# A transformer block in fp32 products: the last modulation group moved into the first down projection, and seven stages of block products in the second

## The chip, the cores and the metric

The kernel runs on one core of a Trainium2 chip. The metric is the device time of one launch in microseconds (us): three runs of the kernel before took 1014.57, 1015.23 and 1015.83, median 1015.23. Names used below: TensorE (PE) multiplies, VectorE (DVE) and ScalarE (ACT) work elementwise, GpSimd (POOL) does little here, SyncE (SP) issues the DMA transfers.

## The reference

One layer over 512 tokens of width 1024: a feed-forward half-step, a token mixer, a second feed-forward half-step. Each is modulated by shift, scale and gate vectors that come from a small vector `c` through a 1024 x 9216 matrix `w_ada`. Everything is float32.

```
sc = jax.nn.silu(c)
mod = sc @ w_ada[l] + b_ada[l]
sh1, s1, g1, sh2, s2, g2, sh3, s3, g3 = jnp.split(mod, N_MOD, axis=-1)
h = _modulate(x, sh1, s1)
x = x + 0.5 * g1[:, None, :] * _swiglu(h, ffn1_w_in[l], ffn1_w_out[l])
h = _modulate(x, sh2, s2)
y = _hybrid_mixer(h, ...)
x = x + g2[:, None, :] * y
h = _modulate(x, sh3, s3)
x = x + 0.5 * g3[:, None, :] * _swiglu(h, ffn2_w_in[l], ffn2_w_out[l])
```

`_modulate` is an RMS norm over the features, times (1 + scale), plus shift. `_swiglu` is `(silu(h @ Wg) * (h @ Wu)) @ w_out` with an inner width of 2816; the second product is the down projection.

## The kernel before

Activations are kept transposed: `xT` is 8 tiles of 128 features x 512 tokens, and the inner activations `act` are 22 tiles (k = 0 to 21) of 128 x 512. A float32 product is made of three matmuls (`mm3`, L475 to L477): each operand is split into a high and a low part, and high x high, high x low and low x high are summed in PSUM. The splits are made by ScalarE (the high part: `ah` of an activation, `wh` of a weight) and VectorE (the low part: `al`, `wl`; L919, L235, L275). Activations that have not been split yet are plain tiles, "whole".

The program has these stages: feed-forward 1, its down projection (`down`, from L1017), the mixer, feed-forward 2, its down projection (`last_down`, from L1152). A down projection makes the 8 tiles of the output, t = 0 to 7, each a sum over 22 k; the weights come in units of 8, 8 and 6 k (`KPARTS`). The update adds the product, times the gate, to `xT[t]` (L1026 in `down`, L1161 in `last_down`; both STT on VectorE).

**Seven stages.** Where two output tiles and 8 k are taken together, a Strassen-Winograd scheme does the 2 x 2 x 2 block product with seven products instead of eight. `seven_down` makes one stage: 7 products of 4 k, each k three matmuls of 128 x 256, that is 84 matmuls. It needs sums and differences of the weights (`sevenths`: in a stage 3 weight remainders of 128 x 1024 and 5 operations of 128 x 512 on VectorE) and of the activations (`act_sums`, L1127 for the differences and L1477 for their low parts: 16 of 128 x 256 and 8 of 128 x 512 for 8 k). These are made of whole activations. In the kernel before, `act[0:8]` are kept whole beside their halves (`self.whole`), and `act[8:16]` exist as high and low parts only: `whole()` in `act_sums` adds them up again (L1133, 8 of them).

**The order of the second down projection** is written out in `PLAN`. Its entries are "all" (all 22 k of a tile), "tail" (only the last 6 k), "most" (the first 8 and the last 6 k), and (0, t) or (1, t): a seven stage over k 0 to 7 or 8 to 15 for tiles t and t+1. Before: tiles 0 and 1 in full, tails of 4 to 7, the stages (0, 4) and (0, 6), tiles 2 and 3 as "most", the stages (1, 2), (1, 4) and (1, 6). Finished tiles are transposed back and stored (`store`, L1294), in between the other work.

**The modulation vectors** beyond the first ones are made in groups of up to four chunks of 512 columns of `w_ada` (`ada_sums`). A chunk is 8 loads of 128 x 512 (256 KB each, issued by SP) and 8 operations of VectorE that multiply by `sc` and add up (L826 for the first, L828 for the 7 others) into a tile `aa`. When a group's chunks are there, `ada_columns` adds over the partitions with one matmul per chunk against ones (L885; each writes 32 rows of one PSUM tile `pb`), ScalarE copies the result (`rw`, L888), after a step TensorE transposes it (L892), and VectorE adds the bias (L896) into `mod`. `ada_rest(groups)` yields after each pair of loads and products, so that the caller can lay it between other work: `side.step(n)` goes n steps on. Group 1 and 2 are made in the first down projection, group 3 (2 chunks: 16 loads, 16 operations of VectorE) in the second, where only its vectors are used.

**The end of the first down projection.** Tile 7 is done in two halves of 256 tokens (`ha`, `hb`), in written order (`in_order`), and the norm of the next stage is begun inside it: ScalarE squares `xT` (L739), VectorE adds the squares to `na` (L741), and six matmuls into the second half TensorE adds `na` over the partitions (L761). Instructions of one engine run in the order in which they stand.

Of the kernel before, what the change touches and what calls it, by code (L numbers as in the profile page):

```python
# [32 lines left out]
PLAN = (("all", 0), ("all", 1), ("tail", 4), ("tail", 5), ("tail", 6), ("tail", 7), (0, 4), (0, 6), ("most", 2), ("most", 3),  # L33
        (1, 2), (1, 4), (1, 6))
MISSING = {"all": (), "most": (1,), "tail": (0, 1)}
# [64 lines left out]
class Block:  # L100
# [814 lines left out]
    def glu_parts(self, a, late=False):  # L915
        nc = self.nc
        ah, al = self.slot(F32R, "ah", late), self.slot(F32R, "al", late)
        nc.scalar.copy(ah, a)
        nc.vector.tensor_tensor(out=al, in0=a, in1=ah.bitcast(F32), op=ALU.subtract)  # L919
        return ah, al  # L920
# [53 lines left out]
    def by_sevens(self, act, fs, others=()):  # L974
# [27 lines left out]
        def parted():  # L1002
            for i in range(last):
                act[i] = self.glu_parts(act[i], 8 <= i < 14)
                yield

        side.add(parted())
        for f in range(last, FT):
            p = []
            for _ in range(2):  # L1010
                u, q = self.next_unit(), self.acc()
                for k in (0, 4):
                    self.dense(q, u, self.h, k0=k, k1=k + 4)
                    side.step(3)
                p.append(q)
            act.append(self.glu(*p))
        self.splits = side  # L1017

    def down(self, act, gate, norm=None):

        nc = self.nc
        accum = self.slot(s="na") if norm else None
# [6 lines left out]
        def finish(t, ts, p):  # L1029
            update(t, ts, p)  # L1030
            if norm:
                self.square_in(t, ts, accum)

        def parts(t, ts, units=None, by=8, late=False):
# [6 lines left out]
            if late:  # L1041
                held.append((t, ts, p))
            elif norm and ts != full:
                update(t, ts, p)
            else:
                finish(t, ts, p)

        last = KT - 1
        side, held = Side(), []
        side.add(self.ada_rest((1, 2) if norm else (3,)))  # L1050
        if norm:
            self.consts = Side()
            self.consts.add(self.mixer_consts())

        def split_first():
# [8 lines left out]
            if norm:  # L1064
                finish(0, full, p)
            else:
                held.append((0, full, p))

        for t in range(last):
            if norm and t == 1:  # L1070
                self.masks()
            for i, _ in enumerate(parts(t, full, late=not norm and t < 2) if t else split_first()):
# [4 lines left out]
                if not norm and t > 2:  # L1077
                    if i == 1:
                        self.store(t - 2, range(NB))
                elif not norm and t == 2:  # L1080
                    if i == 0:
                        side.flush()
                        for h in held:
                            finish(*h)
                    elif i == 1:
                        self.store(0, range(NB))
        units = [self.next_unit(ahead=0) for _ in KPARTS]
        if not norm:
            for i, _ in enumerate(parts(last, ha, units)):
                if i < 2:  # L1090
                    self.store(last - 2 + i, range(NB))
            for i, _ in enumerate(parts(last, hb, units)):
                if i == 1:
                    self.store(last, range(2))
            self.store(last, range(2, 4))
            return None
# [26 lines left out]
    def act_sums(self, tiles):  # L1123
# [5 lines left out]
        def whole(x):  # L1129
            if not isinstance(x, tuple):  # L1130
                return x
            a = self.slot(s="aw")
            tt(out=a, in0=x[0].bitcast(F32), in1=x[1].bitcast(F32), op=ALU.add)  # L1133
# [18 lines left out]
    def last_down(self, act, gate):  # L1152

        nc = self.nc
        full = slice(0, NT)
        side, sums, parts7, ended, held = Side(), Side(), Side(), [], []
        side.add(self.ada_rest((3,)))
# [10 lines left out]
        def stores():  # L1168
            while ended:
                self.store(ended.pop(0), range(NB))  # L1170
                yield

        for at, (kind, t) in enumerate(PLAN):
            after = [k for k, _ in PLAN[at + 1:at + 3]] + ["all"] * 2
            if kind in SEVENS:
# [13 lines left out]
            p = self.acc()  # L1189
            for i, (k0, n) in enumerate(KPARTS):  # L1190
                if i in MISSING[kind]:
                    continue
                u = self.next_unit(ahead=0 if i == 2 and after[0] in SEVENS else 1)
                if kind == "tail" and after[0] == "tail" and after[1] in SEVENS or (
                        i == (0 if kind == "most" else 1) and after[0] in SEVENS):
                    ahead()
                if at == 2:
                    side.flush()
                for k in range(0, n, 2):
                    while not at and any(not isinstance(a, tuple) for a in act[:k0 + k + 5]):  # L1200
                        self.splits.step()
                    for j in range(k, k + 2):
                        xh, xl = act[k0 + j]
                        self.mm3(p, u[0][:, j, :], u[1][:, j, :], xh, xl, k0 + j == (16 if kind == "tail" else 0),
                                 k0 + j == FT - 1)
                    if at == 1:
                        side.step()
                    if at > 1 or i == 2 and at:
                        sums.step()
                    parts7.step()  # L1210
                if ended and kind != "tail":
                    self.store(ended.pop(0), range(NB))
            held.append((t, p))
            if at > 1:
                for h, p in held:
                    update(h, full, p)
                    if kind == "all" or h < 2:
                        ended.append(h)
                held = []
# [80 lines left out]
    def ffn2(self, norms):  # L1300
# [14 lines left out]
        self.by_sevens(act, SEVEN[1])  # L1315
# [1210 lines left out]
```

## Time and profile before

| | before |
|---|---|
| median of 3 runs | 1015.23 us (1014.57 to 1015.83) |
| the profiled execution's own time | 1016.3 us |
| its span in the trace | 1014.6 us |
| TensorE busy | 1003.9 us, 99% of the span |
| VectorE busy | 814.8 us, 80% |
| ScalarE busy | 521.2 us, 51% |
| granted TensorE clock, mean | 1.00 |
| first down projection, tile 5 to the norm's first sum | 332.26 to 373.23 |
| second down projection, first matmul to start of the last seven | 888.70 to 998.57 |

Times in the trace count from the span's start. In the lines that the prediction shows, a window gives its length and then the busy time of each engine with its number of instructions; a row of a timeline gives start, duration, engine, line, operation, and output <- inputs, with xN for N neighbours drawn together, and in brackets how long the engine had been idle and what released it. A row of a group gives count, busy time, mean duration in ns, and the idle time ahead of it. An operation's name stands without its buffer number.

### The profile page before, as it was taken

Reading aid. Unit: us, or ns where it says so; the run is one execution under the profiler, and the core shown is the slowest. Engines: PE = TensorE matmul, PEld = TensorE weight load, DVE = VectorE, ACT = ScalarE, POOL = GpSimd, SP = SyncE. Lnnn points to the kernel's source line nnn. Section 1 sums busy time; section 2 is a strip of 40 time slices with the busy share of each in tenths; the row PEclk is TensorE's granted clock in tenths of the full one; section 3 lists DMA queues with packets and bytes.
Section 4 is the critical chain, followed back from the end, with each engine's and each line's share of the span. In section 5 each row is a group of like instructions: output and inputs, shape, how many; then the busy total and the mean of one; then the engine's idle time right before and its main releaser. Section 6 shows DMA issues by size and latency. Waiting matters only on the chain.

```text
span 1014.6 us, 17859 instructions
## 1 busy us (share of the span) xinstructions
PE 1003.9 (99%) x7029; PEld 906.2 (89%) x7029; DVE 814.8 (80%) x1445; ACT 521.2 (51%) x942; POOL 30.6 (3%) x74
## 2 busy tenths in 40 slices
PE   7999999999999999999999999999999999999998
PEld 6788999999887899888888888999999999987988
DVE  4779999887797847778987649789888888788995
ACT  4454555556422225658756365375555555634443
POOL 0000000000200000100001012000000000000000
PEclk9999999999999999999999999999999999999999
DMA  9863564334588825321132021212333434372612
GB/s 319 295 202 101 170 205 144 107 108 117 172 306 286 299 65 165 102 61 44 48 77 69 24 63 43 83 49 83 99 111 98 116 93 121 107 259 65 177 42 63
DMA packets 204034, 130.84 MB, mean 129 GB/s; under 512 B 14497, under 2 KB 188590, under 8 KB 203950
## 3 DMA queue, kind: packets, MB, share of 16 engines
q1 hardware_dynamic: 203950, 129.70, 42.0%
q8 instruction: 55, 0.90, 0.3%
q14 instruction: 29, 0.24, 0.1%
HBM read 127.18 MB, written 2.49 MB: 128 GB/s over the span
## 4 chain that ended last, share of the span: by engine, by line
PE 92%; DVE 4%; DMA 1%; ACT 1%; SPq 1%; issue 1%; POOL 0%; DVEq 0%; ACTq 0%
PE pa L360 18%; PE pa L475 14%; PE pa L477 14%; PE pa L476 14%; PE pb L360 13%; PE pa L1244 3%; PE pb L1244 2%; DMA ar<-in_w_ada 1%; PE pb L2212 1%; SPq L139 1%; PE pb L475 1%; PE pb L476 1%; PE pb L477 1%; PE pb L2192 1%; PE pb L1749 1%; DVE cv L1693 1%
## 5 line engine op out<-in xcount | busy, mean ns | idle before, releaser
L275 DVE TENSOR_TENSOR wl<-wr,wh 128x1024 fp32r<-128x1024 f32 x114 | 138.6, 1220 | 34.7 <-ACT wh L279 34.4
L234 ACT CAST wh<-wr 128x1024 fp32r<-128x1024 f32 (+1 forms) x81 | 81.0, 1009 | 131.6 <-PE pa L476 118.2
L279 ACT CAST wh<-wr 128x1024 fp32r<-128x1024 f32 x114 | 116.6, 1051 | 22.4 <-DVE wr L275 19.9
L235 DVE TENSOR_TENSOR wl<-wr,wh 128x1024 fp32r<-128x1024 f32 (+1 forms) x81 | 94.1, 1167 | 37.4 <-ACT wh L234 36.1
L475 PE MATMUL pa<-hh,wh 128*128 128x512 f32 (+1 forms) x309 | 119.2, 386 | 0.0
L477 PE MATMUL pa<-hh,wl 128*128 128x512 f32 (+1 forms) x309 | 116.2, 376 | 0.0
L476 PE MATMUL pa<-hl,wh 128*128 128x512 f32 (+1 forms) x309 | 116.1, 376 | 0.0
L475 PE MATMUL pa<-ah,wh 128*128 128x512 f32 (+1 forms) x294 | 110.5, 376 | 0.0
L476 PE MATMUL pa<-al,wh 128*128 128x512 f32 (+1 forms) x294 | 110.0, 374 | 0.0
L477 PE MATMUL pa<-ah,wl 128*128 128x512 f32 (+1 forms) x294 | 109.7, 373 | 0.0
L275 DVE TENSOR_TENSOR wr<-wr,wr 128x512 f32<-128x512 f32 x114 | 78.4, 688 | 1.7
L828 DVE SCALAR_TENSOR_TENSOR aa<-ar,sc,aa 128x512 f32<-128x512 f32 x98 | 73.4, 749 | 7.7 <-DMA ar<-in_w_ada 6.0
L360 PE MATMUL pa<-th,wh 128*128 128x256 f32 x264 | 74.8, 283 | 0.2 <-ACT z L365 0.2
L360 PE MATMUL pa<-hh,wh 128*128 128x256 f32 x264 | 74.8, 283 | 0.0
L360 PE MATMUL pa<-hh,wl 128*128 128x256 f32 x264 | 74.7, 283 | 0.0
L360 PE MATMUL pa<-tl,wh 128*128 128x256 f32 x264 | 74.7, 283 | 0.0
L360 PE MATMUL pa<-th,wl 128*128 128x256 f32 x264 | 74.7, 283 | 0.0
L360 PE MATMUL pa<-hl,wh 128*128 128x256 f32 x264 | 74.7, 283 | 0.0
L475 PEld LDWEIGHTS pa<-hh,wh 128*128 128x128 f32 x309 | 58.4, 189 | 10.1 <-issue 1.6
L477 PEld LDWEIGHTS pa<-hh,wl 128*128 128x128 f32 x309 | 58.2, 188 | 10.1
L475 PEld LDWEIGHTS pa<-ah,wh 128*128 128x128 f32 x294 | 55.3, 188 | 12.2 <-ACT wh L234 2.5
L476 PEld LDWEIGHTS pa<-hl,wh 128*128 128x128 f32 x309 | 58.4, 189 | 8.5
(488 smaller groups left out, 2694.3 us busy)
## 6 DMA issues: line engine op xcount, KB each, us to landing
wr<-in_ffn_w_in SPq DMA_DIRECT2D x79, 512.0 KB
ar<-in_w_ada SPq DMA_DIRECT2D x128, 256.0 KB
wr<-in_ffn_w_out SPq DMA_DIRECT2D x32, 512.0 KB
wr<-in_w_in SPq DMA_DIRECT2D x21, 512.0 KB
wr<-in_ffn_w_out SPq DMA_DIRECT2D x16, 384.0 KB
wr<-in_w_out SPq DMA_DIRECT2D x8, 512.0 KB
wr<-in_ffn_w_in SPq DMA_DIRECT2D x8, 384.0 KB
ar<-in_w_ada SPq DMA_DIRECT2D x6, 512.0 KB
```

What stands on the lines that cost most here:

```text
L139: return self.nc.sync.dma_start(dst, src)
L234: self.nc.scalar.copy(hi, raw)
L235: self.nc.vector.tensor_tensor(out=lo, in0=raw, in1=hi.bitcast(F32), op=ALU.subtract)
L275: sub = lambda out, x, y: nc.vector.tensor_tensor(out=out, in0=x, in1=y, op=ALU.subtract)
L279: nc.scalar.copy(hi[:, :n], raw[:, :n])
L360: nc.tensor.matmul(z, a[:, j, :], b, start=start and j == 0 and i == 0, stop=j == 3 and i == 2, skip_group_check=not start)
L475: mm(out, wh, xh, start=start, stop=False)
L476: mm(out, wh, xl, start=False, stop=False)
L477: mm(out, wl, xh, start=False, stop=stop)
L828: nc.vector.scalar_tensor_tensor(out=acc, in0=a, scalar=sc, in1=acc, op0=ALU.mult, op1=ALU.add)
L1244: nc.tensor.matmul(z, a[:, j, :], b, start=start and j == 0 and i == 0, stop=j == 3 and i == 2, skip_group_check=not start)
L1693: nc.vector.scalar_tensor_tensor(out=a[:, d:], in0=p[:, :NT - d], scalar=wj(3 - d), in1=a[:, d:], op0=ALU.mult, op1=ALU.add)
```

## The change

Three things are changed.

1. Group 3 of the modulation vectors is made in `down` (first down projection), behind groups 1 and 2, and no longer in `last_down`. There the rate of the steps goes from 2 to 3 from tile 4 on. `down` has lost its branch for a second down projection, which nothing called.
2. `PLAN` of the second down projection: "head" (the first 8 k) of tiles 0 and 1, tails of 0, 1 and 2, the stages (0, 2), (0, 4), (0, 6), tails of 3 to 7, the stages (1, 0), (1, 2), (1, 4), (1, 6). That is seven stages instead of five; "all" and "most" are gone. A tile's head and its tail are one sum in PSUM (`begun`).
3. `act[8:16]` stay whole (`left`). Their high and low parts are made between the products of the (0, t) stages (`second`), for the first four of them only the first 256 tokens, since the (1, t) stages need no more of them; the eight additions of `whole()` are gone.

```
-PLAN = (("all", 0), ("all", 1), ("tail", 4), ("tail", 5), ("tail", 6), ("tail", 7), (0, 4), (0, 6), ("most", 2), ("most", 3),
-        (1, 2), (1, 4), (1, 6))
+PLAN = (("head", 0), ("head", 1), ("tail", 0), ("tail", 1), ("tail", 2), (0, 2), (0, 4), (0, 6), ("tail", 3), ("tail", 4),
+        ("tail", 5), ("tail", 6), ("tail", 7), (1, 0), (1, 2), (1, 4), (1, 6))
...
+    def glu_parts(self, a, late=False, ts=slice(0, NT)):
...
+        nc.scalar.copy(ah[:, ts], a[:, ts])
+        nc.vector.tensor_tensor(out=al[:, ts], in0=a[:, ts], in1=ah[:, ts].bitcast(F32), op=ALU.subtract)
...
             for i in range(last):
-                act[i] = self.glu_parts(act[i], 8 <= i < 14)
-                yield
+                if i not in left:
+                    act[i] = self.glu_parts(act[i], i >= 16 if left else 8 <= i < 14)
+                    yield
...
-        side.add(self.ada_rest((1, 2) if norm else (3,)))
+        side.add(self.ada_rest((1, 2, 3)))
...
                 if t:
-                    side.step(4 if not norm else 2)
-                if norm and t == 5:
+                    side.step(2 if t < 4 else 3)
+                if t == 5:
                     self.consts.step()
...
-        def whole(x):
-            if not isinstance(x, tuple):
-                return x
-            a = self.slot(s="aw")
-            tt(out=a, in0=x[0].bitcast(F32), in1=x[1].bitcast(F32), op=ALU.add)
-            return a
...
-            a, b = whole(a), whole(b)
...
-        side.add(self.ada_rest((3,)))
+        whole = act[8:16]
...
+        def second():
+            for i, a in enumerate(whole):
+                act[8 + i] = self.glu_parts(a, ts=l if i < 4 else full)
+                yield
...
-                self.seven_down(w, act, 8 * kind, t, update, work, stores())
+                self.seven_down(w, act, 8 * kind, t, update, work, stores() if kind else halves)
...
-                    sums.add(self.act_sums(act[8:16]))
+                    drain(halves)
+                    sums.add(self.act_sums(whole))
...
-        self.by_sevens(act, SEVEN[1])
+        self.by_sevens(act, SEVEN[1], left=range(8, 16))
```

The instructions stand in a new order at the end of the first down projection and in the second; everywhere else the two programs are alike. In the excerpts `wh`, `wl` are parts of a weight, `ah`, `al` of an activation, `aa` a chunk's sums, `pa`, `pb` PSUM tiles.

TensorE, from the last matmuls of tile 6 to the first of tile 7's first half, before:

```order
L475 MATMUL pa_3858<-ah_3001,wh_3903 128x512
L476 MATMUL pa_3858<-al_3002,wh_3903 128x512
L477 MATMUL pa_3858<-ah_3001,wl_3904 128x512
L885 MATMUL pb_3955<-aa_3513,ones_90 32x512
L885 MATMUL pb_3955<-aa_3618,ones_90 32x512
L885 MATMUL pb_3955<-aa_3702,ones_90 32x512
L885 MATMUL pb_3955<-aa_3802,ones_90 32x512
L475 MATMUL pa_3984<-ah_2906,wh_3933 128x256
```

TensorE six matmuls into tile 7's second half, after:

```order
L475 MATMUL pa_4147<-ah_2910,wh_3998 128x256
L476 MATMUL pa_4147<-al_2911,wh_3998 128x256
L477 MATMUL pa_4147<-ah_2910,wl_3999 128x256
L885 MATMUL pb_4020<-aa_3941,ones_90 32x512
L892 MATMUL pb_4025<-ident_85,rw_4023 128x64 x4
L761 MATMUL pb_4145<-ones_90,na_3005 128x1 x2
L761 MATMUL pb_4146<-ones_90,na_3005 128x1 x2
L475 MATMUL pa_4147<-ah_2914,wh_3998 128x256
```

Before, group 2's four sums stand together ahead of the first half. After, they stand inside tile 6, three together and the fourth 18 rows later; of group 3's two sums the first stands inside the first half, and the second here, with its transposes and the norm's sums of `na` directly behind it.

VectorE around the updates of tile 6 (512 wide) and of tile 7's first half (256 wide), before:

```order
L828 SCALAR_TENSOR_TENSOR aa_3802<-ar_3895,sc_128,aa_3802 128x512
L828 SCALAR_TENSOR_TENSOR aa_3802<-ar_3896,sc_128,aa_3802 128x512
L235 TENSOR_TENSOR wl_3975<-wr_3972,wh_3974 128x768
L1026 SCALAR_TENSOR_TENSOR xT_99<-pa_3858,mod_2360,xT_99 128x512
L741 TENSOR_TENSOR na_3005<-na_3005,sq_3963 128x512
L896 TENSOR_TENSOR mod_4014<-pb_4009,vT_129 128x4x4
L901 TENSOR_SCALAR mod_4014<-mod_4014 128x8
L235 TENSOR_TENSOR wl_4042<-wr_3978,wh_4041 128x1024
```

VectorE around the update of tile 7's first half, after:

```order
L828 SCALAR_TENSOR_TENSOR aa_3941<-ar_3954,sc_128,aa_3941 128x512
L828 SCALAR_TENSOR_TENSOR aa_3941<-ar_3955,sc_128,aa_3941 128x512
L1027 SCALAR_TENSOR_TENSOR xT_99<-pa_4055,mod_2360,xT_99 128x256
L828 SCALAR_TENSOR_TENSOR aa_3941<-ar_3990,sc_128,aa_3941 128x512
L828 SCALAR_TENSOR_TENSOR aa_3941<-ar_3991,sc_128,aa_3941 128x512
L896 TENSOR_TENSOR mod_4030<-pb_4025,vT_129 128x4x2
L741 TENSOR_TENSOR na_3005<-na_3005,sq_4034 128x512
L903 TENSOR_SCALAR mod_4030<-mod_4030 128x8
```

The last two products of group 3 stand behind the update of the first half, and the addition to `na` stands behind the bias addition of group 3's columns; before, all products stood ahead of the update of tile 6, and the addition to `na` ahead of the columns. On ScalarE the square of tile 6 stands directly behind the copy `rw` of group 3.

VectorE in the second down projection, before (at the tile 2 "most", where the weights of stage (1, 2) are prepared):

```order
L275 TENSOR_TENSOR wl_11039<-wr_11024,wh_11038 128x1024
L1477 TENSOR_TENSOR tl_11035<-t_10995,th_11034 128x512
L1133 TENSOR_TENSOR aw_11050<-ah_10220,al_10221 128x512
L1133 TENSOR_TENSOR aw_11052<-ah_10287,al_10288 128x512
L1161 SCALAR_TENSOR_TENSOR xT_99<-pa_10929,mod_10519,xT_99 128x512
L1127 TENSOR_TENSOR t_11054<-aw_11050 128x256
```

And after, in stage (0, 2), where the weights of (0, 4) are prepared:

```order
L275 TENSOR_TENSOR wr_10515<-wr_10515,wr_10516 128x512
L1128 SCALAR_TENSOR_TENSOR xT_99<-pb_10521,mod_4030,xT_99 128x256
L919 TENSOR_TENSOR al_10558<-af_8680,ah_10557 128x256
L275 TENSOR_TENSOR sl_10541<-wr_10516,sh_10540 128x512
L298 TENSOR_TENSOR wr_10516<-wr_10516 128x512
L919 TENSOR_TENSOR al_10594<-af_8806,ah_10593 128x256
```

The additions that rebuilt whole activations are gone from VectorE's queue; in their place stand the low parts of the second eight activations, inside the (0, t) stages.

More of the change, by code (lines that the diff above doesn't have):

```diff
@@ L1015, in by_sevens, with down @@
                 p.append(q)
[L1016 removed]
+            act.append(self.glu(*p, late=bool(left)))
         self.splits = side
[L1019 removed]
+    def down(self, act, gate, norm):
         nc = self.nc
[L1022 removed]
+        accum = self.slot(s="na")
         full, ha, hb = slice(0, NT), slice(0, HALF), slice(HALF, NT)
@@ L1040, in parts @@
                     yield
-            if late:
-                held.append((t, ts, p))
-            elif norm and ts != full:
+            if ts != full:
                 update(t, ts, p)
@@ L1171, in stores @@
                 yield
+        def second():
+            for i, a in enumerate(whole):
+                act[8 + i] = self.glu_parts(a, ts=l if i < 4 else full)
+                yield
+        halves = second()
         for at, (kind, t) in enumerate(PLAN):
-            after = [k for k, _ in PLAN[at + 1:at + 3]] + ["all"] * 2
+            after = [k for k, _ in PLAN[at + 1:at + 3]] + [None] * 2
             if kind in SEVENS:
@@ L1213, in last_down @@
[L1213 to L1219, printed above, removed]
+            p = begun.pop(t, None)
+            start = p is None
+            p = p or self.acc()
+            k0, n = KPARTS[0 if kind == "head" else 2]
+            u = self.next_unit(ahead=0 if after[0] in SEVENS else 1)
+            if after[0] == kind and after[1] in SEVENS:
+                ahead()
@@ new lines, in last_down @@
+            for k in range(0, n, 2):
+                while any(not isinstance(a, tuple) for a in act[k0:k0 + n][:k + 5]):
+                    self.splits.step()
+                for j in range(k, k + 2):
+                    xh, xl = act[k0 + j]
+                    self.mm3(p, u[0][:, j, :], u[1][:, j, :], xh, xl, start and j == 0, k0 + j == FT - 1)
+                if at:
+                    sums.step(2 if kind == "tail" else 1)
+                parts7.step()
+            if kind == "head":
+                begun[t] = p
+            else:
+                update(t, full, p)
```

75 lines of the change are left out of this document (12 added, 63 removed).

## The prediction

> **What bounds the kernel now.** I read the page of the profile first, then the windows (busy time by stretch) of the three places that the change touches, then their timelines. The page's head, its busy times and its chain of waits:
>
> ```profile
> span 1014.6 us, 17859 instructions
> PE 1003.9 (99%) x7029; PEld 906.2 (89%) x7029; DVE 814.8 (80%) x1445; ACT 521.2 (51%) x942; POOL 30.6 (3%) x74
> PE 92%; DVE 4%; DMA 1%; ACT 1%; SPq 1%; issue 1%; POOL 0%; DVEq 0%; ACTq 0%
> ```
>
> TensorE carries 92% of the chain, so a change is worth the matmul time it removes, less every wait that it puts in front of a matmul. The profiled execution took 1016.3 us for a span of 1014.6, 1.07 above the median of 1015.23; I work out differences in the trace and lay them on the median.
>
> The windows: length, then busy time of PE, PEld, DVE, ACT and POOL, granted clock, DMA share, GB/s. The rows are a stretch of plain products in the first down projection, one stage of seven block products in the second, the end of the first down projection (its tile 5 to the first column sum of the norm), the second down projection from its first matmul to its last seven, and two stretches for DMA.
>
> ```profile
> core 0: us, PE busy (x) PEld busy (x) DVE busy (x) ACT busy (x) POOL busy (x), PEclk, DMA share, GB/s
> 285.71:300.67 14.96, 14.96 (x68) 12.39 (x66) 13.18 (x18) 3.49 (x4) 0.00 (x0) 1.00 0.96 321
> 867.71:877.79 10.08, 10.08 (x86) 10.08 (x85) 4.85 (x8) 5.25 (x10) 0.00 (x0) 1.00 0.38 108
> 332.26:373.23 40.97, 40.97 (x220) 34.03 (x218) 27.29 (x41) 9.23 (x12) 1.12 (x32) 1.00 0.64 201
> 888.70:998.57 109.87, 109.87 (x649) 96.61 (x648) 102.01 (x168) 50.09 (x77) 0.00 (x0) 1.00 0.42 128
> 325.00:350.00 25.00, 25.00 (x110) 20.18 (x109) 19.91 (x30) 6.02 (x7) 1.12 (x32) 1.00 0.89 299
> 350.00:375.00 25.00, 25.00 (x158) 21.63 (x158) 13.16 (x20) 4.47 (x6) 0.00 (x0) 1.00 0.45 137
> ```
>
> A plain tile has 66 matmuls of 512 columns: 14.96 / 66 = 0.2267 us each, or 0.68 for one k (three matmuls). A seven has 84 of 256 columns: 10.08 us, the length of its weight loads too. In the second down projection VectorE is busy 102.01 of 109.87 us: it is the engine that can become late there.
>
> **Second down projection: what leaves.** Before, from 888.70 to the start of the last seven, TensorE does two whole tiles (44 k), four tails (24 k), two tiles without their middle part (28 k) and four sevens: 96 x 0.68 + 4 x 10.08 = 105.60. After: two heads (16 k), eight tails (48 k) and six sevens: 64 x 0.68 + 6 x 10.08 = 104.00. That is 1.60 less. The modulation columns leave too; their two places in the timeline (start, duration, then the instruction):
>
> ```profile
> 918.71 1.05 PE L885 MATMUL pb<-aa,ones 128*32 128x512 f32 x4
> 919.70 0.50 PE L475 MATMUL pa<-ah,wh 128*128 128x512 f32 x1
> 919.84 0.58 ACT L888 COPY rw<-pb 64x512 f32<-64x512 f32 x1 [0.41 <-PE pb L885]
> 920.49 0.40 PE L475 MATMUL pa<-ah,wh 128*128 128x512 f32 x1
> 920.82 0.46 PE L892 MATMUL pb<-ident,rw 64*128 64x64 f32 x4
> 921.21 0.50 PE L476 MATMUL pa<-al,wh 128*128 128x512 f32 x1
> ```
>
> The sums hold TensorE 0.99 us (918.71 to 919.70), the transposes 0.5 (920.49 to 921.21 instead of 0.23): 1.5 together. Of the 109.87 that leaves 109.87 - 105.60 - 1.5 = 2.8 for the four stores (16 transposes, the same after) and for small gaps at the joints between the kinds of stage. I take 0.7 of that as gone with the joints. Sum: -1.6 - 1.5 - 0.7 = -3.8; from -3.1 (no gap goes) to -4.3 (1.2 goes). The tail of the program after the last seven stays as it is.
>
> **Whether VectorE keeps up there.** It loses the eight sums that rebuilt whole activations and the group's sixteen steps, and gets two more stages of weights. Rows of the groups in this stretch (count, busy time, mean in ns), then of its timeline, where VectorE runs one operation behind the other:
>
> ```profile
> L1133 DVE TENSOR_TENSOR aw<-ah,al 128x512 f32<-128x512 f32 x8 | 5.1, 683 | 0.0
> L828 DVE SCALAR_TENSOR_TENSOR aa<-ar,sc,aa 128x512 f32<-128x512 f32 x14 | 10.5, 749 | 0.4 <-DMA ar<-in_w_ada 0.2
> L235 DVE TENSOR_TENSOR wl<-wr,wh 128x768 fp32r<-128x768 f32 x2 | 1.9, 948 | 0.0
> 934.08 0.74 DVE L1161 SCALAR_TENSOR_TENSOR xT<-pa,mod,xT 128x512 f32<-128x512 f32 x1
> 934.75 0.42 DVE L1127 TENSOR_TENSOR t<-af 128x256 f32<-128x256 f32 x1
> 935.08 0.69 DVE L275 TENSOR_TENSOR wr<-wr,wr 128x512 f32<-128x512 f32 x1
> 935.68 0.42 DVE L1127 TENSOR_TENSOR t<-af,t 128x256 f32<-128x256 f32 x1
> 936.69 1.22 DVE L275 TENSOR_TENSOR wl<-wr,wh 128x1024 fp32r<-128x1024 f32 x1
> 937.82 0.69 DVE L1477 TENSOR_TENSOR tl<-t,th 128x512 fp32r<-128x512 f32 x1
> 940.82 0.48 DVE L1161 SCALAR_TENSOR_TENSOR xT<-z,mod,xT 128x256 f32<-128x256 f32 x1
> 941.22 1.22 DVE L275 TENSOR_TENSOR wl<-wr,wh 128x1024 fp32r<-128x1024 f32 x1
> ```
>
> Starts lie about 0.08 closer than the durations: 0.67 for a 512-wide update, 0.33 for a 256-wide difference, 0.60 for a 512-wide one, 1.13 for a 1024-wide weight remainder, 0.40 for a 256-wide update; so 0.87 for the 768-wide one. The densest stretch after runs from the start of (0,2) to the start of (1,0): three sevens and five tails, 30.24 + 20.40 = 50.6 us of TensorE. VectorE has there 3 x (3 x 1.13 + 5 x 0.60 weights + 5 x 0.40 + 0.67 updates) = 27.2, the halves of the eight activations 4 x 0.33 + 4 x 0.60 = 3.7, the tails' weights and updates 5 x (0.87 + 0.67) = 7.7, the sums for the second blocks 16 x 0.33 + 8 x 0.60 = 10.1: 48.7 us. It fits with 1.9 us over, and a late remainder is needed only by the product that uses it, 2.9 us or more into a seven. I put no wait there; if the cover is gone, case C has its price.
>
> [...]
>
> **End of the first down projection: what comes in.** The moved group's loads, products, sums and columns now lie among tiles 4 to 7. Before, the last group's columns and what follows ran so:
>
> ```profile
> 363.07 1.06 PE L885 MATMUL pb<-aa,ones 128*32 128x512 f32 x8
> 363.18 0.75 DVE L1026 SCALAR_TENSOR_TENSOR xT<-pa,mod,xT 128x512 f32<-128x512 f32 x1 [2.44 <-PE pa L477]
> 364.06 0.39 PE L475 MATMUL pa<-ah,wh 128*128 128x256 f32 x1
> 364.25 0.59 ACT L888 COPY rw<-pb 128x512 f32<-128x512 f32 x1 [0.21 <-PE pb L885]
> 364.73 0.64 ACT L739 ACTIVATE sq<-xT 128x512 f32<-128x512 f32 x1
> 365.40 0.69 DVE L741 TENSOR_TENSOR na<-na,sq 128x512 f32<-128x512 f32 x1 [1.47 <-ACT sq L739]
> 367.05 0.60 PE L892 MATMUL pb<-ident,rw 128*128 128x128 f32 x4
> 367.68 0.19 DVE L896 TENSOR_TENSOR mod<-pb,vT 128x16 f32<-128x16 f32 x1 [1.59 <-PE pb L892]
> 372.51 0.28 PE L475 MATMUL pa<-ah,wh 128*128 128x256 f32 x1
> 372.71 0.48 DVE L1026 SCALAR_TENSOR_TENSOR xT<-pa,mod,xT 128x256 f32<-128x256 f32 x1 [3.51 <-PE pa L477]
> 373.23 0.95 PE L761 MATMUL pb<-ones,na 128*128 128x1 f32 x8
> ```
>
> Nobody waited: the four L885 took 0.99 (363.07 to 364.06), the copy and the transposes lay under the first half of tile 7, and six matmuls into its second half (372.51 to 373.23) the norm's sum followed at once. What a lone sum costs is not in the trace, but two rows bound it: four sums (x8, two passes each) took 0.99, and two sums (x4, at 918.71) took 0.99 as well. Each writes its own 32 rows of the result and the passes of all of them start together, so the price is one per group, not one per sum. I take 0.99 for a lone one; the other end is a quarter of the four, 0.25.
>
> After, the sums come in four groups instead of one: three, then the fourth of group 2 by itself, then each of group 3's two by itself, one inside the first half of tile 7, one six matmuls into the second half, directly ahead of its transposes and of the norm's sum. I follow that:
>
> - Up to the end of the first half there are two more groups than before, 2 x 0.99, and group 2's transposes, which now lie in tile 6, were there before too; with 0.2 for the restarts 372.51 becomes 374.7. Six matmuls of 0.12: 375.4.
> - VectorE stands at the update of the first half, which needs that half's end: it starts 0.20 behind (372.71 behind 372.51), at 374.9, and takes 0.40. Queued behind it are the last two products of the group, 0.67 + 0.75: 376.7. TensorE's last sum waits for them, 1.4 us that nothing covers, since everything behind it on TensorE's queue waits too.
> - The sum from 376.8 to 377.8. The copy starts 0.19 later and takes 0.59 (364.06, 364.25), the transposes follow at 378.7: 0.9 in which TensorE stands (from 919.70 to 920.82 it was 1.12, with matmuls between).
> - ScalarE's square of tile 6 is queued behind that copy, VectorE's addition to the norm's sum behind the addition of the columns, which starts 0.63 after the transposes (367.05, 367.68) and takes 0.19: 379.4. The addition takes 0.69; the norm's sum follows at 380.1 instead of 373.23, and TensorE has stood another 1.1.
>
> So +6.9: three more groups of sums (2.97) and a second set of transposes with the restarts (0.5) are 3.5 of matmul time; 3.4 are waits in three pieces. Bounds: +5.5, if the two last products run ahead of the update, so that the first of the waits is gone; +8.0, if the copy takes 1.1 and the fourth sum in tile 6 has to wait 0.8 for its row. Everything after hangs on the same chain, shifted.
>
> The DMA cost I put at nothing. Sixteen more loads of 0.26 MB are 4.2 MB, 13 us at 321 GB/s; the stretch from 325 runs at 0.89 of the engines, the one from 350 at 0.45, so they fit by the time of the last products (376), and SP issues them behind weights that it issued before too.
>
> **The sum.** -3.8 + 6.9 = +3.1: the profiled 1016.3 becomes 1019.4, and on the median 1015.23 + 3.1 = 1018.3.
>
> **The rivals.** Within 0.2% (2.03 us, about what a measurement of this kernel can tell from no change) means 1013.2 to 1017.3.
>
> - A, the forecast (0.54): the first down projection loses more at its end than the second gains. 1018.3; with the ends of the terms -4.3 + 5.5 to -3.1 + 8.0, so 1016.4 to 1020.1.
> - B, no change (0.18): the group's last products are done early and the norm's sum finds its addition done; only the 3.5 of matmul time is given back. -3.8 + 3.5 = -0.3: 1014.9. Against it speaks VectorE's queue, which holds two products behind the update of the half.
> - F, faster (0.14): a lone sum, which writes 32 of 128 rows, costs a quarter of the four, 0.25. The three more groups are then 0.75, with transposes and restarts 1.3 instead of 3.5, and the waits are covered as in B. -3.8 + 1.3 = -2.5: 1012.7. It decides from a lone sum under 0.4 us on. Against it: two sums took as long as four. With the waits in place it would be -3.8 + 1.3 + 3.4 = +0.9, 1016.1.
> - C, slower (0.10): VectorE takes full durations, as when each operation waits for a semaphore. Its list for the 50.6 us is then 3 x 10.26 + 4.4 + 5 x 1.70 + 16 x 0.42 + 8 x 0.68 = 56.0, 5.4 late; less 2.9 of cover that is a wait of 2.5 at (1,0): 1018.3 + 2.5 = 1020.8. It decides from a list of 53.5 on. For it: VectorE is already busy 102.01 of 109.87.
> - D, slower (0.04): the loads come late, since SP's queue has the next weights ahead of them; four of them late by 0.8 (0.26 MB at 321 GB/s) give +3: 1021.3. Against it: 0.45 of the engines from 350 on.
>
> **How the numbers follow.** 1018.3 is A's. The range takes in A, B and C, 0.82: 1014.7 to 1020.8. Faster by over 0.2% is F without a part in which the waits stay, with a little of B: 0.14. Of A the part between 1016.4 and 1017.3 lies within 0.2%, about 0.08, and B: 0.26. Slower: the rest of A, C and D: 0.60.
>
> **What would show it.** Right: TensorE's lone L885 take about 1 us each; the gap ahead of the last of them is near 1.4 us, the one ahead of its transposes near 0.9, and the norm's L761 starts 6 to 8 us later than 373.23; the stretch from the second down projection's first matmul to the start of its last seven is near 106.1 us. Wrong: a lone L885 of 0.3 to 0.5 us (F), L761 less than 4 us later (B), that stretch over 108 with weight loads that wait for wl (C), or products that wait for DMA ahead of the last L885 (D).

## The result

The changed kernel takes 1021.97 us (median of 6 runs, 1020.70 to 1024.26), the kernel before 1015.64 beside it (6 runs, 1014.57 to 1016.78). The ratio is 1.0064, 95% interval 1.0051 to 1.0077: 6.5 us slower, between 5.2 and 7.8. The forecast was slower by 3.1; the sign was right, the size was half.

### The profile page after: what moved, and what is told of

It is laid out like the page before. It is cut to its first block, busy times and chain, and to the rows that moved or that the text cites. A ratio compares the mean times of both kernels' runs of the same rounds, so it can differ in the third digit from the quotient of the medians.

```text
span 1019.9 us, 18053 instructions
## 1 busy us (share of the span) xinstructions
PE 1004.6 (99%) x7101; PEld 910.0 (89%) x7101; DVE 822.2 (81%) x1461; ACT 526.5 (52%) x954; POOL 30.6 (3%) x74
## 4 chain that ended last, share of the span: by engine, by line
PE 90%; DVE 5%; DMA 2%; SPq 1%; issue 1%; ACT 1%; POOL 0%; DVEq 0%; ACTq 0%
PE pa L360 18%; PE pb L360 13%; PE pa L475 13%; PE pa L477 13%; PE pa L476 13%; PE pa L1207 4%; PE pb L1207 3%; DMA ar<-in_w_ada 1%; SPq L139 1%; PE pb L2155 1%; PE pb L475 1%; PE pb L476 1%; PE pb L477 1%; DVE cv L1656 1%; PE pb L2175 1%
## 5 line engine op out<-in xcount | busy, mean ns | idle before, releaser
L275 DVE TENSOR_TENSOR wl<-wr,wh 128x1024 fp32r<-128x1024 f32 x120 | 146.1, 1220 | 37.6 <-ACT wh L279 37.2
L234 ACT CAST wh<-wr 128x1024 fp32r<-128x1024 f32 (+1 forms) x77 | 76.8, 1007 | 117.1 <-PE pa L476 95.3
L279 ACT CAST wh<-wr 128x1024 fp32r<-128x1024 f32 x120 | 123.0, 1051 | 26.6 <-DVE wr L275 18.7
L235 DVE TENSOR_TENSOR wl<-wr,wh 128x1024 fp32r<-128x1024 f32 (+1 forms) x77 | 89.2, 1164 | 32.4 <-ACT wh L234 32.0
L475 PE MATMUL pa<-ah,wh 128*128 128x512 f32 (+1 forms) x262 | 98.2, 375 | 0.0
L477 PE MATMUL pa<-ah,wl 128*128 128x512 f32 (+1 forms) x262 | 98.1, 375 | 0.0
L476 PE MATMUL pa<-al,wh 128*128 128x512 f32 (+1 forms) x262 | 98.0, 374 | 0.0
L275 DVE TENSOR_TENSOR wr<-wr,wr 128x512 f32<-128x512 f32 x120 | 82.5, 687 | 1.9
L828 DVE SCALAR_TENSOR_TENSOR aa<-ar,sc,aa 128x512 f32<-128x512 f32 x98 | 72.9, 748 | 5.8 <-DMA ar<-in_w_ada 4.3
L477 PEld LDWEIGHTS pa<-ah,wl 128*128 128x128 f32 x262 | 49.9, 190 | 10.0 <-issue 1.7
```

The costliest lines, as they stand in the source:

```text
L234: self.nc.scalar.copy(hi, raw)
L235: self.nc.vector.tensor_tensor(out=lo, in0=raw, in1=hi.bitcast(F32), op=ALU.subtract)
L275: sub = lambda out, x, y: nc.vector.tensor_tensor(out=out, in0=x, in1=y, op=ALU.subtract)
L279: nc.scalar.copy(hi[:, :n], raw[:, :n])
L475: mm(out, wh, xh, start=start, stop=False)
L476: mm(out, wh, xl, start=False, stop=False)
```

## The profile after, beside that of before

The profiled execution took 1021.56 us, its span is 1019.9, 5.3 longer than before. Head and chain of the page:

```profile
span 1019.9 us, 18053 instructions
PE 1004.6 (99%) x7101; PEld 910.0 (89%) x7101; DVE 822.2 (81%) x1461; ACT 526.5 (52%) x954; POOL 30.6 (3%) x74
PE 90%; DVE 5%; DMA 2%; SPq 1%; issue 1%; ACT 1%; POOL 0%; DVEq 0%; ACTq 0%
```

VectorE's share of the chain has gone from 4 to 5%, TensorE's from 92 to 90: somewhere TensorE waits for VectorE. The windows of the changed kernel: the stretch ahead of the last sum of group 3, the place where it stands, two stretches behind, and the second down projection from its first matmul to the start of its last seven; then 3.40 us out of the third of them, by themselves.

```profile
core 0: us, PE busy (x) PEld busy (x) DVE busy (x) ACT busy (x) POOL busy (x), PEclk, DMA share, GB/s
340.00:375.00 35.00, 35.00 (x183) 27.52 (x182) 27.65 (x45) 5.95 (x7) 1.12 (x32) 1.00 0.79 262
375.00:380.20 5.20, 2.28 (x13) 1.03 (x11) 2.74 (x6) 1.42 (x3) 0.00 (x0) 1.00 0.00 0
380.20:384.40 4.20, 4.14 (x23) 4.17 (x23) 0.00 (x0) 0.00 (x0) 0.00 (x0) 0.59 0.01 4
384.40:390.00 5.60, 5.60 (x49) 5.60 (x49) 3.41 (x8) 2.29 (x4) 0.70 (x1) 1.00 0.20 41
897.64:1003.82 106.18, 106.18 (x713) 98.39 (x712) 100.84 (x167) 55.87 (x90) 0.00 (x0) 1.00 0.33 95
380.84:384.24 3.40, 3.40 (x18) 3.40 (x18) 0.00 (x0) 0.00 (x0) 0.00 (x0) 0.50 0.02 5
```

Two things are to be seen. The second down projection went from 109.87 to 106.18 us, 3.7 less, and TensorE never stands in it. And TensorE stands at the end of the first (busy 2.28 of 5.20 us), and just behind that, at full work again (4.14 of 4.20), it runs at a mean granted clock of 0.59: the column of the clock, the third from the right, is the one that the forecast had no term for. The 0.59 is a mean over the window; the last row shows that the clock is at exactly half for 3.4 us, and the rows around it are at 1.00.

What that costs is read from the same matmuls in both kernels, from the norm's sum to the transposes behind tile 7 (L696), before and after:

```profile
373.23:378.15 4.92, 4.92 (x44) 4.92 (x43) 0.39 (x2) 1.46 (x2) 0.70 (x1) 1.00 0.01 3
380.26:386.80 6.54, 6.54 (x43) 6.54 (x44) 0.44 (x2) 1.05 (x1) 0.70 (x1) 0.74 0.01 3
```

They take 1.6 us longer, and TensorE does not wait among them.

TensorE's timeline of the place where it stands; in brackets how long it was idle, and for whom:

```profile
357.30 1.05 PE L885 MATMUL pb<-aa,ones 128*32 128x512 f32 x2
358.27 0.50 PE L476 MATMUL pa<-al,wh 128*128 128x512 f32 x1
...
375.50 0.28 PE L477 MATMUL pa<-ah,wl 128*128 128x256 f32 x1
377.08 1.04 PE L885 MATMUL pb<-aa,ones 128*32 128x512 f32 x2 [1.31 <-DVE aa L828]
378.86 0.46 PE L892 MATMUL pb<-ident,rw 64*128 64x64 f32 x4 [0.72 <-ACT rw L888]
380.26 1.33 PE L761 MATMUL pb<-ones,na 128*128 128x1 f32 x8 [0.95 <-DVE mod L903]
381.45 0.56 PE L475 MATMUL pa<-ah,wh 128*128 128x256 f32 x1
381.81 0.41 PE L476 MATMUL pa<-al,wh 128*128 128x256 f32 x1
382.02 0.41 PE L477 MATMUL pa<-ah,wl 128*128 128x256 f32 x1
```

VectorE's and ScalarE's rows name what each of the three waits was for:

```profile
375.10 0.48 DVE L1027 SCALAR_TENSOR_TENSOR xT<-pa,mod,xT 128x256 f32<-128x256 f32 x1 [1.41 <-PE pa L477]
375.50 1.53 DVE L828 SCALAR_TENSOR_TENSOR aa<-ar,sc,aa 128x512 f32<-128x512 f32 x2
378.22 0.58 ACT L888 COPY rw<-pb 64x512 f32<-64x512 f32 x1 [11.33 <-PE pb L885]
378.70 0.63 ACT L739 ACTIVATE sq<-xT 128x512 f32<-128x512 f32 x1
379.35 0.17 DVE L896 TENSOR_TENSOR mod<-pb,vT 128x8 f32<-128x8 f32 x1 [2.32 <-PE pb L892]
379.44 0.68 DVE L741 TENSOR_TENSOR na<-na,sq 128x512 f32<-128x512 f32 x1
```

The two last products stand behind the update, the sum waits for them; the transposes wait for the copy; the norm's sum waits for the addition to `na`, which needs the square that was queued behind the copy (the profile names L903, which ended last, but L741 is what L761 reads). The norm's sum starts at 380.26 instead of 373.23, 7.0 later in the trace; counted from the projection's own first matmul (255.79 before, 255.95 after) it is 6.9. A lone sum takes 0.97 (357.30 to 358.27). And the matmuls behind the norm's sum start every 0.21 us, where they started every 0.12 before.

## The experiments

**The theory** (waits and clock): the waits at the end of the first down projection are what was forecast, and because TensorE stands there, its clock drops for some us behind them. **The rival** (later stages): the 3 us that the forecast missed come from the new second down projection or what lies ahead of it, and the clock is incidental. Differences below are medians or ratios against runs of the kernel before on the same chip.

### Group 3 moved alone

The kernel before, with only the first part of the change.

```
-        side.add(self.ada_rest((1, 2) if norm else (3,)))
+        side.add(self.ada_rest((1, 2, 3)))
-                    side.step(4 if not norm else 2)
+                    side.step(2 if t < 4 else 3)
...
-        side.add(self.ada_rest((3,)))
```

> The kernel before with group 3 moved into the first down projection alone (steps 2 and from tile 4 on 3); its second down projection keeps its plan and its order. The theory (waits and clock: TensorE stands in three pieces behind the last lone sum, and its granted clock drops for some us after that): the end of the first down projection costs 7.0 in matmul time and waits and 1.5 or more by the clock, and the second gives back the 1.5 of the columns: 6 to 8 us slower than before, the granted clock between 0.6 and 0.8 for some us just behind the waits. The rival (later stages: what the forecast missed comes from the new second down projection in most executions): 5 us slower or less, 7.0 less 1.5 and the joints.

Measured: 1023.26 against 1015.80, ratio 1.0074 (1.0062 to 1.0087): 7.5 us slower. Windows of the stretch from the transposes on, of the part of it at half clock, of the matmuls from the norm's sum to L696, and of its second down projection:

```profile
378.60:386.30 7.70, 6.75 (x35) 6.64 (x34) 1.01 (x4) 0.58 (x3) 0.70 (x1) 0.56 0.01 2
379.20:386.02 6.82, 6.22 (x29) 6.25 (x30) 0.69 (x3) 0.00 (x0) 0.69 (x1) 0.50 0.01 2
379.80:387.64 7.84, 7.84 (x42) 7.84 (x43) 0.42 (x2) 1.05 (x1) 0.70 (x1) 0.60 0.01 2
898.15:1005.98 107.83, 107.83 (x641) 96.25 (x640) 93.18 (x151) 49.74 (x76) 0.00 (x0) 1.00 0.32 91
```

With the old plan the move loses too, so the new plan isn't needed for the loss, and 7.5 lies where the theory put it. The second down projection gets shorter by 2.0 (109.87 to 107.83) when the columns leave it; from there to the changed kernel's 106.18 the new plan saves another 1.65. The clock is lower than the 0.6 to 0.8 expected: it is at half for 6.8 us, twice as long as in the changed kernel's trace, and the matmuls from the norm's sum to L696 take 7.84 instead of 4.92 us: 2.9 lost.

### The waits filled

First a base: group 3's columns written out where they stood by themselves, so that matmuls can be put between them.

```
+            if g == 3 and q == 0:
+                yield
...
                 if i == 0:
+                    next(self.last_columns)
+                    drain(self.last_columns)
+                    self.square_in(last - 1, full, accum)
                     self.add_sums(pa, accum[:, ha], first=True)
```

> The changed kernel with the columns of group 3 written out at the place where they stood by themselves; one product of the group less stands behind the update of the first half, so that the first wait is 0.8 instead of 1.5 us. It is the base for the run with filling matmuls. The theory (waits and clock): the three waits are 2.8 us together instead of 3.4; 5 to 6 us slower than before if the clock still drops, 4 if these waits are too short for it. The rival (later stages): 0.6 less than the changed kernel, whatever the clock.

Then the same with matmuls in the waits, whose result nothing reads:

```
+                    fill(3)
                     next(self.last_columns)
+                    fill(3)
                     drain(self.last_columns)
                     self.square_in(last - 1, full, accum)
+                    fill(4)
```

> The run with the lone sum, with 3, 3 and 4 matmuls that nothing reads in its three waits (0.7, 0.7 and 0.9 us, so that TensorE's work stands in the waits and makes none of them longer). The theory (waits and clock): the granted clock stays at 1.00 and the time is 1.5 to 2.5 us less than without them, though TensorE does 2.3 us more. The rival (later stages): no change, or up to 0.5 us longer.

Measured: without filling 1022.12, ratio 1.0057 (1.0044 to 1.0069), 5.8 us slower than before; filled 1019.00, ratio 1.0030 (1.0020 to 1.0040), 3.0 slower. TensorE does ten matmuls more and the kernel is 3.1 us faster (2.7 by the ratios), more than the 1.5 to 2.5 expected. The place where TensorE stands, and the matmuls from the norm's sum to L696, without filling:

```profile
375.00:380.20 5.20, 2.85 (x16) 1.64 (x15) 2.08 (x5) 1.53 (x3) 0.00 (x0) 0.87 0.00 0
379.60:387.36 7.76, 7.76 (x43) 7.76 (x44) 0.43 (x2) 1.05 (x1) 0.70 (x1) 0.61 0.01 2
```

and filled, with its second down projection:

```profile
375.00:380.20 5.20, 5.17 (x26) 2.95 (x25) 1.72 (x5) 1.53 (x3) 0.00 (x0) 1.00 0.00 0
379.43:384.43 5.00, 5.00 (x43) 5.00 (x44) 0.44 (x2) 1.05 (x1) 0.70 (x1) 1.00 0.01 3
895.06:1001.26 106.20, 106.20 (x714) 98.42 (x712) 100.87 (x167) 55.92 (x90) 0.00 (x0) 1.00 0.33 95
```

The same matmuls take 7.76 us without filling and 5.00 with it: 2.8 of the 3.1. The waits themselves are still there, only not idle. In this kernel's timeline (its lines for the sum and the transposes are L881 and L890, the filling is L1088) they are seen as filling:

```profile
375.15 0.86 PE L1088 MATMUL pb<-ah,wh 128*128 128x512 f32 x3
375.94 1.05 PE L881 MATMUL pb<-aa,ones 128*32 128x512 f32 x2
376.92 0.97 PE L1088 MATMUL pb<-ah,wh 128*128 128x512 f32 x3
377.81 0.46 PE L890 MATMUL pb<-ident,rw 64*128 64x64 f32 x4
378.20 1.20 PE L1088 MATMUL pb<-ah,wh 128*128 128x512 f32 x4
379.43 1.02 PE L761 MATMUL pb<-ones,na 128*128 128x1 f32 x8
```

The clock stays at 1.00 (0.999 to 1.000 in all nine executions, 0.996 to 0.998 in the five without filling), and what is left is the loss that was forecast: 3.0 against 3.1. The comparison is fair to the changed kernel, although the first wait is shorter here: the filling holds TensorE nearly as long, and the norm's sum comes 124.15 us behind the projection's first matmul (255.28), against 124.31 in the changed kernel and 117.44 before. That is 6.7 more, and less 3.7 it gives the 3.0. The rival falls: the second down projection is 106.20 in the filled kernel too, and from L696 to its start, through mixer and second feed-forward, it is 510.55 us before, 510.84 after and 510.63 filled.

### How much standing it takes

Filled in the third wait only (left standing, by the starts of the rows: 0.7 and 0.7 us), and in the first only (left: 0.7 and 1.3). The expectations took the second wait for 1.0 and so the sums for 1.7, 2.3 and 3.0; in the traces they are 1.4, 2.0 and 2.7.

> The run with the lone sum, with filling matmuls in its third wait only (4, 0.9 us). Of the 3.0 us of standing 1.7 remain, in two pieces of 0.7 and 1.0 within 2.6 us. If the clock drops once the standing adds up to some 2.5 us within 4 (theory A): no drop, as filled in all three, 3.2 us slower than before. If one piece of 1 us is enough (theory B): the drop stays, 6 us slower than before.

> The run with the lone sum, with filling matmuls in its first wait only (3, 0.7 us). Of the 3.0 us of standing 2.3 remain, in two pieces of 1.0 and 1.3, the transposes between them. Theory A (the standing has to add up to some 2.5 us within 4): no drop or a short one, 3 to 4 us slower than before. Theory B (one piece of 1 us is enough): the drop stays, 6 us slower than before.

Measured: the third filled 1019.27, ratio 1.0035 (1.0021 to 1.0049); the first filled 1021.12, ratio 1.0050 (1.0036 to 1.0065). Windows of the 3.41 us ahead of the drop and of the drop, the third filled:

```profile
375.18:378.59 3.41, 2.71 (x18) 2.06 (x18) 0.94 (x3) 1.11 (x2) 0.00 (x0) 1.00 0.00 0
378.59:382.00 3.41, 3.41 (x17) 3.41 (x18) 0.10 (x1) 0.00 (x0) 0.00 (x0) 0.50 0.03 5
```

and the place of the waits and the stretch behind them, the first filled:

```profile
374.92:378.33 3.41, 2.29 (x11) 0.83 (x9) 1.00 (x4) 1.53 (x3) 0.00 (x0) 1.00 0.00 0
379.00:383.00 4.00, 3.97 (x34) 4.00 (x35) 0.16 (x1) 0.33 (x1) 0.70 (x1) 1.00 0.02 4
```

Neither theory A nor theory B holds. In its profiled execution the kernel with less standing (1.4 us) shows a drop, the one with more (2.0) none; but in the five executions the mean clock of the first is 0.998 to 1.000 and that of the second 0.996 to 1.000. So the drop comes or not from one execution to the next. By the ratios the cost over the filled kernel is 0.5 with 1.4 us of standing, 2.0 with 2.0, and 2.7 with all three; that it grows with the standing is not shown, since the intervals of neighbours overlap. TensorE's busy time alone doesn't tell the cases apart either: 2.71 of the 3.41 us ahead of the drop with the third filled, 2.29 of 3.41 with the first filled, where none followed.

The clock was at half for 3.41 us in the traces of the changed kernel and of the third filled, and for 6.8, twice that, in those of the lone sum and of the move alone (6.82 at 0.50 in the latter's row; in the lone sum's trace the four times 2 us from 378.00 on are at 0.70, 0.50, 0.50 and 0.59). No single wait ahead of these drops was over 1.5 us, and the largest sum of them was 3.4 us, with sums and transposes between. Where the limit lies, and what makes a drop short or long, these runs don't settle.

### The columns later

The changed kernel, with the sums and transposes of group 3 deeper in the second half of tile 7.

```
+        self.last_columns = waiting
...
+                if i in (5, 8):
+                    next(self.last_columns, None)
```

> The changed kernel with one edit: the two sums of group 3 and its transposes are written further into the second half of tile 7 (after 36 and after 54 of its 66 matmuls), so that the norm's sum stands in front of them and matmuls lie between the sums and the transposes. Loads and products stay where the change put them. The theory (waits and clock): no wait and no drop of the clock is left; matmul time is 2 groups of sums (1.98) and a set of transposes (0.5) above before, the second down projection gives back 3.8: 1.3 us faster than before, 1014.5. If the loads and products themselves cost something (the rival): slower than before.

Measured: 1015.21 against 1015.28, ratio 0.9998 (0.9990 to 1.0007). The waits, the drop (TensorE is busy 16.00 of 16.00 us from 372 to 388, at 1.00) and with them the changed kernel's loss are gone; but the gain of 1.3 that I expected is not there. Its two rows of columns:

```profile
379.24 1.05 PE L881 MATMUL pb<-aa,ones 128*32 128x512 f32 x4
382.56 0.46 PE L888 MATMUL pb<-ident,rw 64*128 64x64 f32 x4
```

I had priced a group of sums at 0.99. With the restart ahead of it (0.21 from the last matmul's start instead of 0.12) and the one behind (0.22 instead of 0.12) it is 1.18, and a set of transposes 0.55: 2 x 1.18 + 0.55 = 2.9 above before, less 3.7: -0.8, inside the interval.

### All steps earlier

```
-                    side.step(2 if t < 4 else 3)
+                    side.step(3)
```

> The changed kernel with one number changed: the steps of the groups go at 3 from tile 1 on, not at 2 up to tile 3. In the order the products of group 3 then stand ahead of the update of tile 6 and its columns inside tile 6, so that the norm's sum has nothing in front of it. The theory (the loss comes from the standing behind the last products and the clock after it): no wait and no drop; what stays of 7.0 is matmul time, three more groups of sums (2.97, 0.3 for each restart) and the transposes (0.5), about 4.2, less the 3.7 of the second down projection: within 1 us of before. The rival (the loads have no room: the DMA engines are at 0.96 in tiles 2 and 3): products and weights wait for DMA there, 3 us or more slower than before.

Measured: 1019.06 against 1016.04, ratio 1.0030 (1.0018 to 1.0042): 3.0 us slower. The theory was right that no wait is left, and no drop in the trace (1.00 in every window from 270 to 390), and wrong on the time; the rival had the time, but its mechanism is out: TensorE does not wait (no gap of over 0.13 us from 243 to 385). The sums of this kernel:

```profile
305.93 1.06 PE L885 MATMUL pb<-aa,ones 128*32 128x512 f32 x6
307.59 1.05 PE L885 MATMUL pb<-aa,ones 128*32 128x512 f32 x2
...
333.31 1.05 PE L885 MATMUL pb<-aa,ones 128*32 128x512 f32 x4
335.18 1.04 PE L885 MATMUL pb<-aa,ones 128*32 128x512 f32 x2
344.56 1.05 PE L885 MATMUL pb<-aa,ones 128*32 128x512 f32 x2
...
364.34 1.04 PE L885 MATMUL pb<-aa,ones 128*32 128x512 f32 x2
367.13 1.04 PE L885 MATMUL pb<-aa,ones 128*32 128x512 f32 x2
```

Three sums (x6), two (x4) and one (x2) all take 1.04 to 1.06. Ten sums lie in seven groups, where before eight lay in two: 5 x 1.18 + 0.55 = 6.5, less 3.7 is +2.8. I had counted only the groups of group 3 as new. This kernel shows the matmul part of the loss without any wait.

### Group 3 beside the second feed-forward

New plan and whole activations as in the change, but group 3 beside the sevens of the second feed-forward, where one stage keeps VectorE busy 4.85 of 10.08 us.

```
-        side.add(self.ada_rest((1, 2, 3)))
+        side.add(self.ada_rest((1, 2)))
-                    side.step(2 if t < 4 else 3)
+                    side.step(2)
-        self.by_sevens(act, SEVEN[1], left=range(8, 16))
+        self.by_sevens(act, SEVEN[1], (self.ada_more((12, 13), [], 3),), left=range(8, 16))
```

> The new plan and the whole activations, with group 3 neither in the first nor in the second down projection but beside the sevens of the second feed-forward, where VectorE is busy for half the time; first down projection as before. The theory (waits and clock, and a second down projection that gains by its count): 1.6 less by the sevens and 0.7 by the joints, the columns' 1.5 paid where they now are: 2.3 us faster than before, 1013.3, the clock at 1.00. The rival (later stages cost about 2 us in most executions): no faster than before.

And the same place for group 3 with the old plan:

> The kernel before with group 3 beside the sevens of the second feed-forward, with its own plan and its rebuilt activations. If the gain of the run with the new plan and the same place for group 3 (1.3 us) comes from the plan: within 0.5 us of before. If it comes from the place of group 3 (VectorE and the joints freed in the second down projection): 0.7 to 1.3 us faster than before.

Measured: with the new plan 1014.51 against 1015.80, ratio 0.9986 (0.9977 to 0.9995), 1.4 faster; with the old plan 1015.36 against 1015.28, ratio 0.9997 (0.9988 to 1.0006), within 0.5 of before, as expected if the gain comes from the plan. The second down projection, new plan:

```profile
889.35:995.83 106.48, 106.31 (x714) 98.41 (x713) 100.90 (x167) 55.94 (x90) 0.00 (x0) 1.00 0.33 94
```

and old plan:

```profile
889.75:997.60 107.85, 107.85 (x642) 96.30 (x640) 93.18 (x151) 49.64 (x76) 0.00 (x0) 1.00 0.31 91
```

Between these two kernels only the plan and the kept activations differ: 107.85 - 106.48 = 1.4 us, where the count of matmuls gave 1.6; in the new plan's trace TensorE waits 0.2 of it (busy 106.31 of 106.48). From 109.87 to 107.85 are 2.0 for the columns and the joints, where I had 1.5 + 0.7. The kernel with the new plan beats both given kernels. Its gain of 1.4 is less than the 2.3 expected, and the far end of the interval, in part because the columns that it still pays cost 1.18 + 0.55 = 1.7 and not 1.5; -3.4 + 1.7 = -1.7.

## Why the prediction was half right

- **Second down projection, -3.8**: right. 109.87 to 106.18 is -3.7; the sevens 1.65 of 1.60 (107.83 to 106.18, the move alone against the changed kernel), columns and joints 2.0 of 2.2 (109.87 to 107.83). VectorE kept up: no matmul waited for it (TensorE busy 106.18 of 106.18), and case C (2.5 us at (1, 0)) did not come. There are operations that cost their full duration (in the trace of before the L828 at 338.48 starts 0.03 behind the end of the L826 whose result it reads, 337.64 and 0.81), but in this stretch VectorE ran as priced (the L275 at 923.39 starts 0.09 ahead of the end of the L1128 at 923.00, 0.48). (C's list adds up to 55.8, not 56.0.)
- **A lone sum costs as much as four, 0.99**: right, 0.97 and 0.98; case F is out. The price of a group with its restarts is 1.18.
- **First down projection, +6.9 in matmul time and three waits**: right. Counted from the projection's first matmul the norm's sum is 6.9 later. (The upper bound's two terms, 0.5 and 0.8, add up to +8.2, not +8.0.) The waits were forecast at 1.4, 0.9 and 1.1; from the starts of the rows they are 1.5 (375.50 to 377.08, less 0.12), 0.8 and 1.1.
- **DMA at nothing**: right, from 300 to the norm's sum no product waited for its load, ahead of that four in this projection (1.8 us together, the longest 0.6; before five, 2.8 and 1.0), and the three waits above are the only ones of TensorE in it; case D is out.
- **"Everything after hangs on the same chain, shifted"**: this step failed. What follows the waits was not shifted, it was slowed: the granted clock was at half for 3.4 us in the profiled execution, and the matmuls behind the waits took 1.6 us longer. The other five executions have a mean clock of 0.996 to 0.998, where the kernel before has 0.999 to 1.000; the two kernels whose profiled executions have 0.996 and 0.997 lose 2.9 and 2.8 there, with the clock at half for 6.8 us. So the forecast's 3.1 becomes 4.7 with the short drop and about 6 with the long one, against 6.5 (5.2 to 7.8) measured. That the untraced executions lost their time at the same place is inferred from their mean clock. The filling shows the cause: with the clock held up the kernel loses 3.0.
- **The range**, 1014.7 to 1020.8, had no case in which the time behind a wait has a price of its own; with 1.6 to 2.9 for it the forecast of 1018.3 would have been 1019.9 to 1021.2.

Single traces have to be compared by stage and not by their spans: kernels that are alike up to the norm's first sum have it at 373.23 (before), 372.41 and 371.57 (the two kernels with group 3 beside the second feed-forward), because the first down projection already starts at 255.79, 254.95 and 254.11. By stage the 5.3 between the spans of before and after are 0.2 ahead of the first down projection, 6.9 up to the norm's sum, 1.6 at the slow clock, 0.3 between there and the second down projection, and -3.7 in it. The 0.3 is not followed up.

## What to carry to other kernels

Where a change makes TensorE stand in a place where it had never stood, price the waits, and then price the clock behind them: look at the granted clock behind each cluster of waits, and don't take waits for harmless because each is short: here three of 0.8 to 1.5 us, close together, were followed by 1.6 us of loss at a granted clock of 0.50, and in two other kernels by 2.8 and 2.9. Work that is moved "beside" other work still has a chain of its own, product, sum, copy, transpose, addition, and its last links should have other work between them, on every engine's queue that they pass; the same columns a few us later in the order cost no wait at all. Sums of 32 rows that run together had the price of one here, so a scheduler that pulls them apart has a cost that the count of instructions doesn't show.

## What the runs showed of the hardware

- Matmuls against ones that write 32 rows each ran at once: the first passes of four started within 0.02 us (363.07 to 363.09, before), and one, two, three or four of them took 0.97 to 1.00 us together, 1.18 with the restarts.
- TensorE standing in pieces of 0.7 to 1.5 us, 1.4 to 3.4 in all within 5 us, was followed by 3.4 or 6.8 us at a granted clock of 0.50 in the traces of four kernels, and by none in that of a fifth (2.0 us of standing). The matmuls behind took 1.6 us longer with the 3.4 of the changed kernel, 2.8 and 2.9 with the 6.8. Ten matmuls that nothing reads, in these pieces, made the kernel 3.1 us faster.
